# Contiguous step sizes, an earlier routing chain, and a bias table built inside the expert loop of a one-core decoder layer

## The chip, the cores and the metric

The kernel runs on one core of a Trainium2 chip. TensorE (PE) multiplies, VectorE (DVE), ScalarE (ACT) and GpSimd (POOL) do the elementwise work, and 16 DMA engines move data between device memory and the on-chip memory; SyncE (SP) issues most transfers, GpSimd the indirect ones (gather and scatter by row number). Each engine works through its own queue in order and waits at the head of it. The metric is the device time of one execution in microseconds (us), as the median of several runs.

## The reference

One decoder layer over 512 tokens of width 1024. A projection feeds a state-space branch (S5: 32 groups of 64 complex states, whose step sizes are exp of `ssm_log_step`, one number for each group) and a pooling branch with windows 2, 4, 8 and 16; both are gated, merged, projected, and added to the input in a layer norm. Then follow a mixture of 32 experts, 4 for each token, and a per-layer embedding:

```python
step = jnp.exp(log_step.astype(f32))[:, None]
lam_bar = jnp.exp(lam * step)
...
logits = (t @ w_router + b_router).astype(jnp.float32)
top_val, top_idx = lax.top_k(logits, TOP_K)
weights = jax.nn.softmax(top_val, axis=-1)
...
g = xb @ w_gate[e] + b_gate[e]
u = xb @ w_up[e] + b_up[e]
g = jnp.minimum(g, SWIGLU_LIMIT)
u = jnp.clip(u, -SWIGLU_LIMIT, SWIGLU_LIMIT)
glu = g * jax.nn.sigmoid(SWIGLU_ALPHA * g)
return ((u + 1.0) * glu) @ w_down[e] + b_down[e]
...
ple = jax.nn.sigmoid(h @ w_ple_gate[i]) * (p[i] @ w_ple_proj[i])
h = _layer_norm(DEEPNORM_ALPHA * h + moe_out + ple, ln2_g[i], ln2_b[i])
```

## The kernel before

The program has three stages. Ahead of the expert loop the order of each engine's queue is made at compile time by the tile framework's scheduler: it plays the program through with its own estimates of durations and gives each engine, whenever it is free, the ready instruction that comes first in the program's text. On the chip that order is fixed, and an instruction whose operand is late holds everything behind it. From `with tc.manual_schedule():` on (the expert loop) each engine keeps the order of the text among the loop's own instructions; where these fall among the instructions written before the loop is still the scheduler's choice.

**Front.** The 1024 x 3072 input projection and the other weights of this stage are loaded as 512 KB tiles (`load_raw`), and each tile is split into a high and a low half (`split`: the high half on ScalarE, the difference on VectorE, L104), so that three matmuls (`mm3`, L115 to L117) give nearly full precision. Line 167 loads the step sizes `lsb`: two transfers, each for 64 partitions, in which partition p of half g2 gets elements g2, g2+2, g2+4, ... of the 32 numbers. On VectorE a chain of some hundred small instructions on the tile `sm` makes the recurrence's coefficients from `par` and `lsb`. GpSimd makes tables of powers (`eb`, `er`, `ei`, L286 to L291) from them, VectorE uses these in the scan (`q_state`), and between them VectorE makes the pooling branch's `ph` (`pool_vec`), which PE multiplies at once.

**Routing and embedding.** After the output projection, each of four token tiles is normalized (`ln_vec`), stored to device memory as `hd`, and transposed into `hTs` (`ln_T`; tiles `ahi`, `alo`). `route_mm` makes the router's logits, `route_vec` transposes them (L764), adds the bias (`lg`, L767), finds the top four, ranks the experts by load (`key`, `cmp`, `col`), and makes the list row of every (token, choice), `ri` (L813). GpSimd writes 16 indirect scatters (L817) into the lists `lst`, and five loads bring these back as `ls` and `ls4` (L997, L1000). `ix4` (L1003) turns `ls4` into row numbers for the later scatter-adds. `route_cols` finds which expert has which rank (`eid`), makes `ib` (L855), and gathers the bias rows of all experts with four indirect transfers (L859) into `br`, from which ScalarE and VectorE make the table `btab` (L863, L864). Meanwhile PE computes the embedding in two halves of 512 columns: `ple_g` (L922 to L924) and L1079 to L1081 for the gate, `ple_p` (L939 to L941) for the projection; `ple_w` and `ple_wp` load and split its weights, VectorE multiplies and adds (`ple_mul`, `base_b`, `base_out`), and L957 stores the sum to `acc_d`.

**Expert loop.** 32 experts in a fixed order of their rank, each with three weights of 4 MB in four tiles of 1 MB; tile k of the stream goes into slot k of a ring of 16:

```python
ring += [(p_, "eraw", 1) for p_ in (ra, rb, rd, rg, rc, rf, re_)] + [(mtop, "eraw", 4)] * 4
...
for n in range(NR):
    do_load(n)
for i in range(2):
    gather(xgs[i], ls[:, i], CAP[i])
```

Five slots have memory of their own; the other eleven reuse memory of the stages before, so that their first load waits for the last instruction that reads the old tile. The four of `mtop` lie where `hTs` was. An expert's tokens are gathered from `hd` by the list (L1016), transposed (`half_T`, L1009, L1010) and multiplied (L1125). The bias comes from one matmul with `btab` (L1208): for the first expert behind its fourth weight tile, for the others ahead of the first. Results go by scatter-add to `acc_d` (L1160). The last expert is combined on PE, and the final layer norm closes the program.

Of the kernel before, what the change touches and what calls it, by code (L numbers as in the profile page):

```python
# [26 lines left out]
GP = G // 2  # L27
# [10 lines left out]
NB = 4  # L38
# [30 lines left out]
def _layer(top, tc, nc, x, xT, pT, ssm, ssm_d, log_step, w_in, w_val, w_glg, w_pg, pscale, w_pp,  # L69
# [96 lines left out]
    for g2 in range(2):  # L166
        nc.sync.dma_start(lsb[g2 * 64:(g2 + 1) * 64],
                          bass.AP(tensor=log_step.tensor, offset=log_step.offset + g2, ap=[[0, 64], [2, GP]]))
    dsk = sp.tile([32, GP], F32, name="dsk")
# [591 lines left out]
    def route_vec():  # L761
# [50 lines left out]
        V.tensor_reduce(rk, o2, axis=AX.X, op=OP.add)  # L812
        V.tensor_copy(ri, rk)  # L813
        scat = []
        for t_ in range(4):
            for k in range(K):
# [4 lines left out]
                scat.append(q_)  # L821
        tt(o2, oh, b4(wk), OP.mult)
        V.tensor_reduce(m1, o2.rearrange("p t k e -> p t e k"), axis=AX.X, op=OP.add)
# [5 lines left out]
    eid = late.tile([1, E], I32, name="eid")  # L829
    ib = mide.tile([128, 2], I32, name="ib")  # L830
    rowb = mide.tile([1, 2, NB, E], BF16, name="rowb")

    def route_cols():
# [21 lines left out]
        V.tensor_copy(ib, pb[:, 0:4].rearrange("p (h a) -> p h a", a=2)[:, :, 0])  # L855
        for h_ in range(2):
            br = mid.tile([128, 512], F32, tag="sg", name="br", bufs=4)
            for m_, b_ in enumerate((b_gate, b_up)):
                P.indirect_dma_start(out=br[:, m_ * 256:(m_ + 1) * 256], out_offset=None, in_=b_.rearrange("e (j c) -> (e j) c", j=NB),  # L859
                                     in_offset=bass.IndirectOffsetOnAxis(ap=ib[:, h_:h_ + 1], axis=0),  # L860
                                     bounds_check=NB * E - 1, oob_is_err=False)
            bh_ = mide.tile([128, 512], F32R, tag="bh", name="bh", bufs=1)
            S.copy(bh_, br)  # L863
            stt(btab[:, :, h_], bh_.bitcast(F32).rearrange("p (m c) -> p m c", m=2), odd, br.rearrange("p (m c) -> p m c", m=2), OP.mult, OP.add)  # L864

# [45 lines left out]
    def ple_w(n0):  # L911
        PW[n0] = [wtile(w_pleg, 2 * i, 2, n0 * 512, 512, P if n0 == 0 and i in (1,) else None) for i in range(4)]

# [62 lines left out]
    ple_g(0, 1)  # L976
    ln_T(3)
    route_mm()
    ple_g(0, 2)
    route_vec()  # L980

# [20 lines left out]
    ix4 = late.tile([128, NB, E], I32, name="ix4")  # L1002
    ts(ix4, ls4[:, :, :, 0], float(NB), OP.mult, jc, OP.add)  # L1003

# [15 lines left out]
    ple_g(0, 3)  # L1020
    route_cols()
    cn = mide.tile([128, 4, NB, E], BF16, name="cn")
    for r_ in range(NB):
        V.tensor_copy(cn[:, :, r_], mk)
    NC_ = N_CAND
# [27 lines left out]
    for t_ in range(4):  # L1053
        ple_p(0, t_, sacc())
        ple_mul(0, t_)
    ple_w(1)
    ple_wp(1)
    route_w()
# [145 lines left out]
    def bias(m_, c):  # L1204
        def f(os, start=True, stop=False):
            for i in range(len(os)):
                n_ = min(2, CAP[c] // 32 - 2 * i)
                TE.matmul(os[i][:, :256 * n_], lhsT=SL[c], rhs=btab[:, m_, c // 16, None, :].to_broadcast([128, n_, 256]),  # L1208
                          start=start, stop=stop, skip_group_check=True)
        return f  # L1210

    def raw_load(src, q_, down):
# [157 lines left out]
    with tc.manual_schedule():  # L1370
        for n in range(NR):
            do_load(n)
        for i in range(2):
            gather(xgs[i], ls[:, i], CAP[i])
        X[0] = x_tile()
        SL[0] = sel_e(0)
        for i in range(2):
            half_T(xgs[0], X[0], i, CAP[0], (S.copy, V.tensor_copy)[i])
        P.indirect_dma_start(out=tab, out_offset=bass.IndirectOffsetOnAxis(ap=bx[:NC_, 0:1], axis=0),
                             in_=bx[:NC_, 1:3], in_offset=None, bounds_check=NC_ - 1, oob_is_err=False)  # L1380
        n = 0
        for i in range(E + 1):
            for s in range(12):
# [4 lines left out]
                if i == E and s == 2:  # L1388
                    gb = tail_load(fin)
                if here:  # L1390
                    _, m_, q_ = seq[n]
                    w_ = raws.pop(n)
                    if m_ == 2:
                        c = ORD[i - 1]
                        last = i == E
                        if q_ == 0:
                            PY[c] = [acc(), acc()] if last else [sacc() for _ in banks(c)]
                        if last:
                            mm_rows(PY[c], HT[c], w_, q_, CAP[c])
                        else:  # L1400
                            mm_tile(PY[c], HT[c], w_, q_, nb_of(c), True, True)
                    else:
                        c = ORD[i]
                        os = (PG, PU)[m_][c]
                        mm_tile(os, X[c], w_, q_, nb_of(c), i == 0)
                        if i == 0 and q_ == 3:
                            bias(m_, c)(os, False, True)
                    do_load(n + NR)
                    n += 1
# [89 lines left out]
def _lay_out(inp):  # L1499
# [10 lines left out]
    r["ssm_d"] = c(a["ssm_d"].reshape(GP, 2, H).transpose(1, 2, 0).reshape(2 * H, GP))  # L1510
    r["log_step"] = c(a["ssm_log_step"].reshape(G))
    r["pool_scale"] = c(a["pool_scale"].reshape(4, 128).T)
# [17 lines left out]
```

## Time and profile before

| | |
|---|---|
| median of 3 runs (lowest, highest) | 1517.55 us (1516.02, 1518.83) |
| the profiled execution | 1518.69 us, span 1517.0 us |
| TensorE busy | 1356.2 us (89%) |
| VectorE, ScalarE, GpSimd busy | 438.2, 245.5, 287.7 us |
| read from and written to device memory | 453.23 MB, 17.80 MB |
| mean granted TensorE clock | 0.97 |

The span runs from the first to the last instruction in the trace; the execution's own time is 1.7 us longer. In the rows below, times are in us from the span's start, and a second number is a duration. `tile<-tiles` names what an instruction writes and reads, x5 counts merged instructions, and brackets hold the idle time of the engine before it and what ended that. PE, PEld, DVE, ACT, POOL are TensorE's matmuls and weight loads, VectorE, ScalarE, GpSimd; SPq and POOLq are the queues that issue transfers. A row of windows gives the stretch, its length, the busy time of PE, PEld, DVE, ACT and POOL, then the granted TensorE clock, the busy share of the DMA engines and GB/s. A row of waits gives the total, the number and the longest.

### The profile page before, as it was taken

To read this page: it belongs to the slowest core of one execution; us is meant where nothing else is said; L and a number is where in the kernel's file an instruction comes from. 1 tells how busy PE (TensorE), PEld (TensorE's weight loads), DVE (VectorE), ACT (ScalarE), POOL (GpSimd) and SP (SyncE) were. 2 spreads that over 40 slices of the span, in tenths; PEclk is the share of its full clock that TensorE was granted. 3 is DMA by queue.
4 is the path that set the end of the run, shared out by engine and by line. 5 is a ranking of instruction groups with operands and counts; after the bars stand their busy time and mean duration, and the time that the engine had idled before them with its cause. 6 is when DMAs were issued, how large, how long until landed. Compare 5 with 4: busy or idle time off the path is not lost.

```text
span 1517.0 us, 41208 instructions
## 1 busy us (share of the span) xinstructions
PE 1356.2 (89%) x18454; PEld 877.0 (58%) x18454; DVE 438.2 (29%) x940; ACT 245.5 (16%) x436; POOL 287.7 (19%) x293
## 2 busy tenths in 40 slices
PE   6779999999699999998989889989898899999993
PEld 6658887777455666554545445545454455556651
DVE  3986747587311111110111111101110111111106
ACT  2434334242100011000010000000100000000011
POOL 0294310002501112111112111111121111110132
PEclk9889999999899999999999999999999999999997
DMA  4412325730599999999999999999999999999953
GB/s 153 136 55 72 93 85 201 210 126 24 220 403 398 397 400 385 386 399 397 395 400 393 393 386 392 401 394 394 393 393 391 382 391 400 397 383 408 409 181 140
DMA packets 107780, 468.58 MB, mean 309 GB/s; under 512 B 19757, under 2 KB 44785, under 8 KB 58448
## 3 DMA queue, kind: packets, MB, share of 16 engines
q1 hardware_dynamic: 90864, 446.12, 75.3%
q0 software_dynamic: 16736, 19.79, 6.0%
q8 instruction: 146, 2.39, 0.6%
q14 instruction: 34, 0.28, 0.0%
HBM read 453.23 MB, written 17.80 MB: 311 GB/s over the span
## 4 chain that ended last, share of the span: by engine, by line
DMA 56%; PE 30%; DVE 5%; issue 4%; POOL 3%; ACT 0%; SPq 0%; DVEq 0%; ACTq 0%; POOLq 0%
DMA eraw<-in_w_down_dram 23%; DMA eraw<-in_w_up_dram 15%; DMA eraw<-in_w_gate_dram 14%; PE acc L1125 10%; PE ss L1125 5%; PE acc L116 3%; PE acc L117 3%; PE acc L115 3%; DMA lsb<-in_log_step_dram 2%; POOL lst L817 1%; PE acc L1132 1%; PE tp L1141 1%; DMA raw<-in_w_out_dram 1%; DMA lst<-dfl 1%; DVE eraw L191 1%
## 5 line engine op out<-in xcount | busy, mean ns | idle before, releaser
L1125 PE MATMUL acc<-eraw,xt 128*32 128x256 f32 x10880 | 608.7, 382 | 47.8 <-DMA eraw<-in_w_up_dram 45.4
L1125 PEld LDWEIGHTS acc<-eraw,xt 128*32 128x32 f32 x10880 | 347.2, 110 | 297.1 <-DMA eraw<-in_w_up_dram 65.8
L1125 PE MATMUL ss<-eraw,ht 128*32 128x256 f32 x5312 | 303.1, 383 | 31.4 <-DMA eraw<-in_w_down_dram 31.4
L1160 POOL DMA_INDIRECT acc_d<-y,ix x83 | 129.5, 1560 | 868.8 <-ACT y L1194 852.9
L1125 PEld LDWEIGHTS ss<-eraw,ht 128*32 128x32 f32 x5312 | 171.5, 111 | 158.6 <-DMA eraw<-in_w_down_dram 45.2
L1142 ACT COPY ht<-tp 128x512 f32<-128x512 f32 (+1 forms) x50 | 23.9, 516 | 649.9 <-PE tp L1141 649.9
L181 DVE TENSOR_SCALAR g<-acc 128x512 f32<-128x512 f32 (+1 forms) x51 | 30.6, 602 | 286.7 <-PE acc L1125 276.2
L1010 DVE COPY xt<-tp 128x384 f32<-128x384 f32 (+2 forms) x32 | 16.4, 511 | 332.1 <-PE tp L1009 332.0
L183 DVE TENSOR_SCALAR u<-acc 128x512 f32<-128x512 f32 (+1 forms) x51 | 30.6, 600 | 274.0 <-PE acc L1125 265.4
L115 PE MATMUL acc<-ahi,hi 128*128 128x512 f32 x160 | 64.3, 402 | 15.1 <-DVE sm L191 15.1
L1175 ACT ACTIVATE s<-g 128x512 f32<-128x512 f32 (+1 forms) x51 | 27.9, 559 | 282.4 <-DVE g L181 282.4
L104 DVE TENSOR_TENSOR lo<-raw,hi 128x1024 fp32r<-128x1024 f32 (+1 forms) x52 | 63.0, 1215 | 28.8 <-ACT hi L103 28.5
L103 ACT CAST hi<-raw 128x1024 fp32r<-128x1024 f32 (+1 forms) x53 | 54.9, 1036 | 72.6 <-PE acc L116 48.8
L117 PE MATMUL acc<-ahi,lo 128*128 128x512 f32 x160 | 63.9, 399 | 0.0
L116 PE MATMUL acc<-alo,hi 128*128 128x512 f32 x160 | 63.7, 398 | 0.0
L115 PEld LDWEIGHTS acc<-ahi,hi 128*128 128x128 f32 x160 | 31.0, 194 | 21.6 <-ACT hi L103 15.4
L1016 POOL DMA_INDIRECT xg<-hd,ls x32 | 32.4, 1014 | 34.4 <-PE tp L1009 24.9
L117 PEld LDWEIGHTS acc<-ahi,lo 128*128 128x128 f32 x160 | 30.8, 192 | 6.6
L116 PEld LDWEIGHTS acc<-alo,hi 128*128 128x128 f32 x160 | 30.9, 193 | 6.2
L1194 ACT ACTIVATE y<-ss,ls 128x256 f32<-128x256 f32 x83 | 33.8, 481 | 0.0
L187 DVE TENSOR_TENSOR g<-g,s 128x512 f32<-128x512 f32 (+1 forms) x51 | 29.2, 600 | 13.1 <-ACT s L1175 13.1
L191 DVE SCALAR_TENSOR_TENSOR u<-u,g 128x512 f32<-128x512 f32 (+1 forms) x51 | 30.8, 603 | 1.7
(404 smaller groups left out, 1301.3 us busy)
## 6 DMA issues: line engine op xcount, KB each, us to landing
eraw<-in_w_gate_dram SPq DMA_DIRECT2D x128, 1024.0 KB
eraw<-in_w_up_dram SPq DMA_DIRECT2D x128, 1024.0 KB
eraw<-in_w_down_dram SPq DMA_DIRECT2D x128, 1024.0 KB
raw<-in_w_in_dram SPq DMA_DIRECT2D x23, 512.0 KB
raw<-in_w_out_dram SPq DMA_DIRECT2D x8, 512.0 KB
raw<-in_w_ple_gate_dram SPq DMA_DIRECT2D x8, 512.0 KB
raw<-in_w_pool_proj_dram SPq DMA_DIRECT2D x4, 512.0 KB
raw<-in_w_glu_val_dram SPq DMA_DIRECT2D x4, 512.0 KB
```

The lines of the kernel that those rows point to most:

```text
L103: S.copy(h, v)
L104: (lo_eng or V).tensor_tensor(l, v, h.bitcast(F32), op=OP.subtract)
L115: TE.matmul(o, lhsT=lh, rhs=rh, start=start, stop=False)
L116: TE.matmul(o, lhsT=lh, rhs=rl, start=False, stop=False)
L117: TE.matmul(o, lhsT=ll, rhs=rh, start=False, stop=stop)
L181: V.tensor_scalar(o, i, a, None, op0=op)
L183: V.tensor_scalar(o, i, a, b, op0=op, op1=op1)
L191: V.scalar_tensor_tensor(o, a, s, b, op0=op0, op1=op1)
L1016: P.indirect_dma_start(out=xg[:n_], out_offset=None, in_=hd, in_offset=bass.IndirectOffsetOnAxis(ap=lst_[:n_, 0:1], axis=0), bounds_check= ...
L1125: TE.matmul(os[b // 2][j * 32:(j + 1) * 32, b % 2 * 256:b % 2 * 256 + 256], lhsT=x_, rhs=w_[:, kk, j * 256:(j + 1) * 256], start=first and ...
L1160: q_ = P.indirect_dma_start(out=acc_d.rearrange("t (j c) -> (t j) c", j=4), out_offset=bass.IndirectOffsetOnAxis(ap=ix_[b], axis=0), in_=y ...
L1194: S.activation(y_[:, b * 256:(b + 1) * 256], py[b // 2][:, c_], AF.Copy, scale=w_.bitcast(F32))
```

## The change

`log_step` is stored as two rows of 16 on the host, so that each partition loads one contiguous row. `ln_T(3)`, `route_mm` and `route_vec` get the highest priority of the scheduler. `route_vec` ends with the scatters; its former last part (the weights of each choice for the down bias) becomes `route_w3`. What VectorE does for `route_w3`, `route_cols`, the copies `cn` and the second half of the embedding's weights is ordered behind `ri`. Two of the four low halves of these weights, up to now all VectorE's, go to GpSimd. The bias gathers and `btab` move from `route_cols` into the first step of the expert loop, in two larger tiles of the loop's own memory; `ib` moves to a pool that lives on, and one buffer of 2 KB for each partition is gone. `ix4` moves from ahead of the embedding's rest into the loop's text, behind the first gathers.

```diff
--- before.py
+++ after.py
@@ -164,8 +164,7 @@
     nc.sync.dma_start(par, ssm)
     lsb = sp.tile([128, GP], F32, name="lsb")
     for g2 in range(2):
-        nc.sync.dma_start(lsb[g2 * 64:(g2 + 1) * 64],
-                          bass.AP(tensor=log_step.tensor, offset=log_step.offset + g2, ap=[[0, 64], [2, GP]]))
+        nc.sync.dma_start(lsb[g2 * 64:(g2 + 1) * 64], bc(log_step[g2], 64))
     dsk = sp.tile([32, GP], F32, name="dsk")
     nc.sync.dma_start(dsk, ssm_d)
 
@@ -810,7 +809,8 @@
         tt(o2, oh, rv[:, :, None, :].to_broadcast([128, 4, K, E]), OP.mult)
         rk = mide.tile([128, 4, K], F32, name="rk")
         V.tensor_reduce(rk, o2, axis=AX.X, op=OP.add)
-        V.tensor_copy(ri, rk)
+        RT["ri"] = V.tensor_copy(ri, rk)
+        RT["m1"], RT["wk"] = m1, wk
         scat = []
         for t_ in range(4):
             for k in range(K):
@@ -819,7 +819,11 @@
                 for o_ in scat:
                     tc.declare_no_dep(q_.ins, o_.ins, reason="each (token, choice) has a list row of its own")
                 scat.append(q_)
-        tt(o2, oh, b4(wk), OP.mult)
+
+    def route_w3():
+        o2, oh = (RT["s"][:, i].rearrange("p (t k e) -> p t k e", t=4, k=K) for i in range(2))
+        m1, wk = RT["m1"], RT["wk"]
+        tt(o2, oh, wk[:, :, :, None].to_broadcast([128, 4, K, E]), OP.mult)
         V.tensor_reduce(m1, o2.rearrange("p t k e -> p t e k"), axis=AX.X, op=OP.add)
         S.copy(w3[:, :, 0], m1)
         S.copy(w3[:, :, 2], m1)
@@ -827,7 +831,7 @@
         RT["w3"] = w3
 
     eid = late.tile([1, E], I32, name="eid")
-    ib = mide.tile([128, 2], I32, name="ib")
+    ib = late.tile([128, 2], I32, name="ib")
     rowb = mide.tile([1, 2, NB, E], BF16, name="rowb")
 
     def route_cols():
@@ -853,15 +857,6 @@
         for h_ in range(2):
             TE.matmul(pb[:, 2 * h_:2 * h_ + 2], lhsT=ir.rearrange("p e j a -> p (e j a)")[:, h_ * 128:(h_ + 1) * 128], rhs=one[0:1, 0:2], start=True, stop=True)
         V.tensor_copy(ib, pb[:, 0:4].rearrange("p (h a) -> p h a", a=2)[:, :, 0])
-        for h_ in range(2):
-            br = mid.tile([128, 512], F32, tag="sg", name="br", bufs=4)
-            for m_, b_ in enumerate((b_gate, b_up)):
-                P.indirect_dma_start(out=br[:, m_ * 256:(m_ + 1) * 256], out_offset=None, in_=b_.rearrange("e (j c) -> (e j) c", j=NB),
-                                     in_offset=bass.IndirectOffsetOnAxis(ap=ib[:, h_:h_ + 1], axis=0),
-                                     bounds_check=NB * E - 1, oob_is_err=False)
-            bh_ = mide.tile([128, 512], F32R, tag="bh", name="bh", bufs=1)
-            S.copy(bh_, br)
-            stt(btab[:, :, h_], bh_.bitcast(F32).rearrange("p (m c) -> p m c", m=2), odd, br.rearrange("p (m c) -> p m c", m=2), OP.mult, OP.add)
 
     def route_w():
         pt = tps()
@@ -909,7 +904,7 @@
     PW = {}
 
     def ple_w(n0):
-        PW[n0] = [wtile(w_pleg, 2 * i, 2, n0 * 512, 512, P if n0 == 0 and i in (1,) else None) for i in range(4)]
+        PW[n0] = [wtile(w_pleg, 2 * i, 2, n0 * 512, 512, P if i in ((1,), (0, 1))[n0] else None) for i in range(4)]
 
     def ple_g(n0, t_):
         c_ = slice(t_ * 128, (t_ + 1) * 128)
@@ -974,10 +969,11 @@
     ple_g(0, 0)
     ln_T(2)
     ple_g(0, 1)
-    ln_T(3)
-    route_mm()
+    with tc.high_priority():
+        ln_T(3)
+        route_mm()
+        route_vec()
     ple_g(0, 2)
-    route_vec()
 
     rn = [0]
 
@@ -1000,7 +996,6 @@
         P.dma_start(ls4[j * 32:(j + 1) * 32].rearrange("s b e w -> s b (e w)"),
                     lst[:128 * E].rearrange("(b s e) w -> s b (e w)", s=32, e=E))
     ix4 = late.tile([128, NB, E], I32, name="ix4")
-    ts(ix4, ls4[:, :, :, 0], float(NB), OP.mult, jc, OP.add)
 
     def half_T(src, o_, q_, n_=128, cp=S.copy):
         pt = tps()
@@ -1018,10 +1013,13 @@
                              bounds_check=T - 1, oob_is_err=False)
 
     ple_g(0, 3)
-    route_cols()
+    with tc.issue_after(RT["ri"].ins):
+        route_w3()
+        route_cols()
     cn = mide.tile([128, 4, NB, E], BF16, name="cn")
-    for r_ in range(NB):
-        V.tensor_copy(cn[:, :, r_], mk)
+    with tc.issue_after(RT["ri"].ins):
+        for r_ in range(NB):
+            V.tensor_copy(cn[:, :, r_], mk)
     NC_ = N_CAND
     cps = tps()[:NC_, :2]
     ones2 = one[:, 0:2]
@@ -1053,8 +1051,9 @@
     for t_ in range(4):
         ple_p(0, t_, sacc())
         ple_mul(0, t_)
-    ple_w(1)
-    ple_wp(1)
+    with tc.issue_after(RT['ri'].ins):
+        ple_w(1)
+        ple_wp(1)
     route_w()
     og = [acc() for _ in range(4)]
     order = (0, 1, 2, 3)
@@ -1208,6 +1207,21 @@
                 TE.matmul(os[i][:, :256 * n_], lhsT=SL[c], rhs=btab[:, m_, c // 16, None, :].to_broadcast([128, n_, 256]),
                           start=start, stop=stop, skip_group_check=True)
         return f
+
+    def bias_rows():
+        br = mz.tile([128, D], F32, tag="u2", name="br", bufs=2).rearrange("p (h m c) -> p h m c", h=2, m=2)
+        for h_ in range(2):
+            for m_, b_ in enumerate((b_gate, b_up)):
+                P.indirect_dma_start(out=br[:, h_, m_], out_offset=None, in_=b_.rearrange("e (j c) -> (e j) c", j=NB),
+                                     in_offset=bass.IndirectOffsetOnAxis(ap=ib[:, h_:h_ + 1], axis=0),
+                                     bounds_check=NB * E - 1, oob_is_err=False)
+        return br
+
+    def bias_table(br):
+        bh_ = mz.tile([128, D], F32, tag="y", name="bh", bufs=2).rearrange("p (h m c) -> p h m c", h=2, m=2)
+        S.copy(bh_.bitcast(F32R), br)
+        for h_ in range(2):
+            stt(btab[:, :, h_], bh_[:, h_], odd, br[:, h_], OP.mult, OP.add)
 
     def raw_load(src, q_, down):
         r = raw_tile()
@@ -1372,10 +1386,12 @@
             do_load(n)
         for i in range(2):
             gather(xgs[i], ls[:, i], CAP[i])
+        ts(ix4, ls4[:, :, :, 0], float(NB), OP.mult, jc, OP.add)
         X[0] = x_tile()
         SL[0] = sel_e(0)
         for i in range(2):
             half_T(xgs[0], X[0], i, CAP[0], (S.copy, V.tensor_copy)[i])
+        br = bias_rows()
         P.indirect_dma_start(out=tab, out_offset=bass.IndirectOffsetOnAxis(ap=bx[:NC_, 0:1], axis=0),
                              in_=bx[:NC_, 1:3], in_offset=None, bounds_check=NC_ - 1, oob_is_err=False)
         n = 0
@@ -1387,6 +1403,8 @@
                 hooks(i, s)
                 if i == E and s == 2:
                     gb = tail_load(fin)
+                if i == 0 and s == 2:
+                    bias_table(br)
                 if here:
                     _, m_, q_ = seq[n]
                     w_ = raws.pop(n)
@@ -1508,7 +1526,7 @@
     cc = [a[f"ssm_c_{s}"].reshape(GP, 2, H, PS).transpose(1, 3, 0, 2).reshape(128, GP * H) for s in ("re", "im")]
     r["ssm"] = c(np.concatenate(lam + b + cc, axis=1))
     r["ssm_d"] = c(a["ssm_d"].reshape(GP, 2, H).transpose(1, 2, 0).reshape(2 * H, GP))
-    r["log_step"] = c(a["ssm_log_step"].reshape(G))
+    r["log_step"] = c(a["ssm_log_step"].reshape(GP, 2).T)
     r["pool_scale"] = c(a["pool_scale"].reshape(4, 128).T)
     for k in ("w_in", "w_glu_val", "w_glu_gate", "w_pool_group", "w_pool_proj", "w_out", "ln1_g", "ln1_b",
               "w_router", "b_router", "w_gate", "b_gate", "w_up", "b_up", "w_down", "b_down", "w_ple_gate",
```

## Rows read from the trace of the kernel before

**Rows 1.** The chain that ended last, whole run: start, length, work.

```profile
12.92 24.12 DMA lsb<-in_log_step_dram
...
278.79 8.91 DMA lst<-dfl
...
364.84 1.18 POOL lst L817
...
385.85 5.07 DMA lst<-pay,ri
```

**Rows 2.** Windows of the late part: busy time of each engine, granted clock, DMA.

```profile
398.30:412.40 14.10, 13.13 (x55) 10.44 (x55) 9.12 (x15) 3.88 (x7) 6.42 (x9) 0.82 0.39 127
...
411.00:469.00 58.00, 55.90 (x946) 33.72 (x949) 11.18 (x24) 3.76 (x8) 3.86 (x5) 0.97 1.01 401
...
469.00:1363.00 894.00, 814.76 (x13900) 477.64 (x13888) 116.11 (x222) 81.31 (x182) 138.26 (x98) 0.99 1.02 393
```

**Rows 3.** SyncE's queue, 340 to 480 us, who waited for whom.

```profile
SPq L1217 <- PE tp L1009: 30.1, 1, 30.1
```

**Rows 4.** Who waited for whom, 0 to 125 us.

```profile
DVE sm L183 <- DMA lsb<-in_log_step_dram: 18.5, 1, 18.5
...
PE acc L115 <- DVE sm L191: 15.1, 1, 15.1
...
PE tp L116 <- DVE ph L187: 11.4, 1, 11.4
```

**Rows 5.** VectorE's timeline, routing stage: start, length, line, tiles, idle time before.

```profile
349.49 0.29 DVE L187 TENSOR_TENSOR lg<-tp,brt 128x128 f32<-128x128 f32 x1 [7.45 <-PE tp L764]
...
352.32 1.22 DVE L104 TENSOR_TENSOR lo<-raw,hi 128x1024 fp32r<-128x1024 f32 x1
...
360.88 1.22 DVE L187 TENSOR_TENSOR cmp<-cmp,ie 128x1024 f32<-128x1024 f32 x1
...
363.73 0.16 DVE L813 CAST ri<-rk 128x16 int32<-128x16 f32 x1
...
396.12 0.33 DVE L183 TENSOR_SCALAR ix<-ls,jc 128x128 int32<-128x128 int32 x1 [13.93 <-DMA ls<-lst]
```

**Rows 6.** VectorE's timeline in the front.

```profile
37.14 0.17 DVE L183 TENSOR_SCALAR sm<-lsb 128x16 f32<-128x16 f32 x1 [18.51 <-DMA lsb<-in_log_step_dram]
...
45.30 0.68 DVE L161 COPY v_u<-acc 128x512 f32<-128x512 f32 x1
```

**Rows 7.** TensorE's timeline in the front.

```profile
30.65 0.40 PE L117 MATMUL acc<-hi,alo 128*128 128x512 f32 x1
```

**Rows 8.** The page's 40 slices of the span, TensorE's busy tenths.

```profile
PE   6779999999699999998989889989898899999993
```

**Rows 9.** ScalarE's timeline, routing stage.

```profile
345.51 0.58 ACT L759 COPY rs<-tp 64x512 f32<-64x512 f32 x1 [4.30 <-PE tp L756]
```

**Rows 10.** TensorE's timeline, 336 to 372 us.

```profile
349.00 0.46 PE L764 MATMUL tp<-ident,rs 64*128 64x64 f32 x4
```

**Rows 11.** All engines' timeline, 318 to 325 us.

```profile
320.46 2.39 POOL L104 TENSOR_TENSOR lo<-raw,hi 128x1024 fp32r<-128x1024 f32 x1 [43.58 <-DVE lni L183]
...
320.93 1.93 DVE L187 TENSOR_TENSOR lnwk<-lni 128x1 f32<-128x1 f32 x1
...
324.79 0.15 DVE L187 TENSOR_TENSOR lnwk<-lnwk 128x1 f32<-128x1 f32 x1
```

**Rows 12.** TensorE's timeline, 372 to 424 us.

```profile
398.30 0.80 PE L939 MATMUL tp<-wp,pth 128*128 128x512 f32 x1 [13.45 <-DVE h L191]
...
409.39 0.39 PE L1081 MATMUL acc<-hi,alo 128*128 128x512 f32 x1
...
412.43 10.82 PE L1125 MATMUL acc<-eraw,xt 128*32 128x256 f32 x192
```

**Rows 13.** GpSimd's timeline, 318 to 420 us.

```profile
397.30 1.25 POOL L859 DMA_INDIRECT br<-in_b_gate_dram,ib  x1 [0.30 <-DVE h L187]
```

**Rows 14.** VectorE's timeline, 383 to 440 us.

```profile
404.95 0.75 DVE L191 SCALAR_TENSOR_TENSOR btab<-bh,odd,br 128x512 fp32r<-128x512 f32 x1 [1.24 <-ACT bh L863]
```

## The prediction

> **What bounds the kernel now.** I read the chain that ended last first, then the windows, then the waits of each engine. The chain [rows 1] names two early places where nothing else could go on. The load of the step sizes alone stands on it for 24.12 us from 12.92. Then come 16 list scatters on POOL, from 364.84 to the landing at 385.85 + 5.07 = 390.92. Behind them it is mostly the stream of expert weights, and the windows [rows 2] say why: from 411 to 1363 the DMA engines are full (1.01 and 1.02, 393 to 401 GB/s) while PE has 79 us of slack in the second window (894 less 814.76). So the loop's length is that of its weights, and what can be won lies before 411, the moment when the stream starts again. SyncE says what holds it until then: one load waited 30.1 us for PE [rows 3]. It waits for memory that the embedding's matmuls (names ahi, lo) still read; the ring's last slots come free only with them. Whatever moves the end of these matmuls (409.39 + 0.39 = 409.78, [rows 12]) and the first expert matmul (412.43) moves the end of the kernel, one for one.
>
> Two stages stand before that. In the front [rows 4] VectorE idles 18.5 us for the step sizes, PE idles 15.1 us behind that (its next operands are split on VectorE, in order), and 11.4 us once more for ph. In the routing stage VectorE's timeline [rows 5] shows the second knot: the first logits add at 349.49, the row numbers ri at 363.73, other work between them, and at 396.12 the one small row ix, before which VectorE stood 13.93 us for the lists. All the embedding's remaining work was queued behind ix: PE waits 13.45 us in turn [rows 12].
>
> **The change part by part. Step sizes.** 2 x 64 partitions x 16 elements are 2048 pieces of 4 bytes; 24.12 us is 11.8 ns for one. Now there are 128 rows of 64 bytes. No row shows such a load. From below: 128 x 11.8 ns = 1.5 us, landing at 14.4. From above: 128 rows of 2 KB took 8.91 us [rows 1], landing at 21.8. VectorE was ready for them at 37.14 - 18.51 = 18.63 [rows 6], so the wait left is 0 to 3.2 us; I take 0, since 64 bytes lie nearer to 4 than to 2048. The Trainium skill (DMA: Bandwidth & Descriptors, Specifications) wants 512 bytes or more for line rate, which 64-byte rows still miss; by it the load stays slow per byte, and the rival on a wait that stays is its case. That hangs on no number here.
>
> What takes the wait's place? VectorE's order has v_u, a copy of PE's first sums, 45.30 - 37.14 = 8.2 us behind the first use [rows 6]. It would come at 26.8, and PE's sums end at 30.65 + 0.40 = 31.05 [rows 7]: up to 4.2 us are lost if the order stays. From below the front gives 18.5 - 3.2 - 4.2 = 11.1 us. From above, PE's two waits go together, 15.1 + 11.4 = 26.5 us. I take 18.5: the two waits for POOL's products apart, VectorE works without a break from the step sizes to ph, where PE's second wait ends, and from the fourth of the page's 40 slices to the tenth PE is at 9 tenths [rows 8], so a shift there is kept.
>
> **Routing chain first.** The transposes of the logits start at 349.00 [rows 10] although their operand was ready at 345.51 + 0.58 = 346.09 [rows 9]; PE had embedding matmuls in between. Put first: 2.9 us. On VectorE, between 349.49 and 363.73, the change moves out two splits (1.22 busy, 1.13 from start to start; the second covered a wait for PE, so I count half), three passes over the 1024-wide comparison at 1.13 [rows 5] and three small copies (0.1 each): 1.1 + 0.6 + 3.4 + 0.3 = 5.4 us. Together 8.3 us. The moved work costs nothing where it goes: VectorE is idle from 382 to 396 and PE sets the pace.
>
> Against it: two of the second half's splits go from VectorE to POOL. The one split that POOL does now took 2.39 us [rows 11], and the 128 x 1 multiply that VectorE started in its midst took 1.93 us against 0.15 for its like. Two such meetings inside the routing chain cost up to 2 x 1.8 = 3.6 us, none cost nothing. The Trainium skill (SBUF — State Buffer, Who interferes with whom) has this as a rule: a VectorE instruction with two SBUF inputs and a GpSimd instruction that reads SBUF exclude each other. By it the chain loses the 3.6 us if both splits fall into it; the row agrees. I take 0.3, since the splits wait for buffers that embedding matmuls free late. So the lists come 8.0 us earlier, at 388.
>
> **Bias table.** Four gathers leave POOL's queue, two casts ScalarE's and two VectorE passes leave the stretch before the first expert. They cost the end nothing now: the embedding's matmuls on PE end at 409.78, after the table (404.95 + 0.75 = 405.70, [rows 14]). In the loop's first step the table is needed behind four weight tiles, 10.82 us after PE starts [rows 12]. Today's set takes from 397.30 [rows 13] to 405.70, 8.4 us; the cover holds if the gathers start no later than 2.4 us after PE does. They wait for memory that only embedding matmuls read, so they can. If late, PE loses that much, out of its slack. I count 0; losing the cover costs 0 to 8 us of PE and, for the end, what exceeds the loads already waiting, which I leave at 0 to 2.
>
> **The row ix.** It moves behind all embedding work in the program's text, but the compiler's scheduler still decides where it falls in VectorE's queue, and no row shows that. If it falls behind the embedding, the hold of VectorE goes, and with it at most PE's 13.45 us and the half-speed after it (granted clock 0.82 over 14.1 us, 2.5 us): 15.9 us, which then includes the 8.0. If it still falls in front, the embedding resumes when the lists land, and the stage gains just the 8.0 us. If it falls earlier, by as much as the routing chain moved forward, PE stands before more work: I put 4 us of the 8 back, which is 4. Bounds 3 and 15.9. I take 8.0, the middle case.
>
> Memory: the smaller pool shifts others by 2 KB; I count 0.
>
> **The sum.** 18.5 + 8.0 = 26.5 us. The profiled execution took 1518.69 us (span 1517.0 and 1.7 around it), which gives 1492.2; it stood 1.1 us above the median of 1517.55, so I forecast 1491 for the median.
>
> **Rivals.** (a) ix no longer holds anything: 18.5 + 15.9 = 34.4, 1483. For it: the new place in the text; against: the scheduler fills idle VectorE time, and lists that it takes as early stood in front this time too. (b) ix falls earlier: 18.5 + 4 = 22.5, 1495. For it: the routing chain, and with it the expected lists, move forward against the embedding. (c) PE's second front wait goes too: 26.5 + 8.0 = 34.5, 1483; against: POOL's part of the chain is no shorter. (d) The front wait is replaced (late 64-byte rows, v_u in front, another load): between 0 and 11 us, with 8.0 in the middle stage between 1498.5 and 1509.5. The step sizes then do not do what the change says. (e) Slower or level, by one mechanism: ix falls right behind ri, at 355.7. VectorE is then held until 388 with nearly all of the embedding behind it. PE has from 355.7 to 384.85 (29.2 us) and from 398.30 to 412.43 (14.1 us) of work left, so its experts start at 388 + 43.3 = 431.3, 18.9 us later than today; against 18.5 from the front that is 1518, and with PE also waiting for VectorE's 2 to 3 us of evacuations 1520 to 1521. It decides from there on: each us that ix falls later gives one back.
>
> **How the numbers follow.** Forecast 0.41, (a) 0.18, (b) 0.17, (c) 0.10, (d) 0.07, (e) 0.04, and 0.03 for gains that two new waits together eat up. Low end: 26.5 + 15.9 = 42.4, 1475. High end: 11.1 + 3 = 14.1, 1503.5. Inside lie the forecast, (a), (b), (c) and half of (d); the joint extremes and (e) are left out, under 2 in 10. This kernel can tell 0.2%, about 3 us, from no change: the forecast and (a) to (d) are faster, 0.93; same 0.03; (e) is the slower 0.04.
>
> **What would show it.** Right: no VectorE wait for lsb, PE without the gap at 31; ri about 9 us behind the first logits add (14.2 now); the lists near 370 and the first expert matmul near 386; the loop from the stream's start to the end as long as today. Wrong: a new wait at v_u or at a weight load near 30; a POOL split in front of the scatters; ix with more than 14 us of idle time before it; a bias matmul that PE waits for; or a loop that grows, which no term here allows for.

## The result and the profile after

The changed kernel takes 1494.65 us (median of 4 runs, 1493.64 to 1496.11) against 1516.86 us of the kernel before (4 runs): a ratio of 0.9852, 95% interval 0.9835 to 0.987, that is 22 us faster. The forecast was 1491.0 with 26.5 us of gain, the range 1475 to 1503.5. The profiled execution after took 1496.11 us, its span 1494.4.

The front first, VectorE's timeline of the changed kernel (start, duration, instruction, in brackets the idle time before it and what ended that); it answers to [rows 6]:

```profile
19.02 0.11 DVE L182 TENSOR_SCALAR sm<-lsb 128x16 f32<-128x16 f32 x1
...
27.12 0.68 DVE L161 COPY v_u<-acc 128x512 f32<-128x512 f32 x1
```

The first use of the step sizes has no wait in front of it and starts 18.1 us earlier. The copy v_u has none either. Of the waits [rows 4] only the last is left, as long as before (total, number, longest):

```profile
PE tp L116 <- DVE ph L186: 11.6, 1, 11.6
```

The routing chain on VectorE, in the order of [rows 5]:

```profile
326.61 0.29 DVE L186 TENSOR_TENSOR lg<-tp,brt 128x128 f32<-128x128 f32 x1 [4.74 <-PE tp L763]
...
334.53 2.02 DVE L186 TENSOR_TENSOR rs<-rs,rv 128x512 f32<-128x512 f32 x1
...
337.31 1.54 DVE L812 CAST ri<-rk 128x16 int32<-128x16 f32 x1
...
373.68 0.47 DVE L182 TENSOR_SCALAR ix<-ls,jc 128x128 int32<-128x128 int32 x1 [9.34 <-DMA ls<-lst]
```

From lg to ri it takes 10.7 us instead of 14.24. The product rs and the cast ri are slow here, 2.02 and 1.54 us. POOL shows why (its timeline), and also where the bias gathers now stand:

```profile
333.59 5.23 POOL L104 TENSOR_TENSOR lo<-raw,hi 128x1024 fp32r<-128x1024 f32 x2 [30.43 <-ACT hi L103]
339.14 1.37 POOL L817 DMA_INDIRECT lst<-pay,ri  x1 [0.32 <-DVE ri L812]
...
380.77 1.07 POOL L1215 DMA_INDIRECT br<-in_b_gate_dram,ib  x1 [0.32 <-issue]
```

The scatters start at 339.14, 25.7 us before the 364.84 of [rows 1]. VectorE still idles 9.34 us in front of ix, but all eight sums that free TensorE's banks now stand ahead of it. TensorE's timeline shows what follows; it answers to [rows 12]:

```profile
377.15 0.39 PE L1080 MATMUL acc<-hi,alo 128*128 128x512 f32 x1
...
380.76 10.57 PE L1124 MATMUL acc<-eraw,xt 128*32 128x256 f32 x192
400.90 1.01 PE L1207 MATMUL acc<-btab,sel_e 128*128 128x512 f32 x2 [9.57 <-DVE btab L190]
401.84 13.07 PE L1124 MATMUL acc<-eraw,xt 128*32 128x256 f32 x192
```

The wait of 13.45 us is gone, the embedding ends 32.2 us earlier and the first expert starts 31.7 us earlier. Then there is a new wait, 9.57 us for the bias table. The chain that ended last shows the same gathers as one of its pieces:

```profile
384.77 14.15 DMA br<-in_b_up_dram,ib
```

The last stretch starts where TensorE's chain switches from waiting for weights to its own work, at 1340.24 (1363.01 before): 22.8 us. So 31.7 us at the first expert became 22.8 at the end, and the first question is where the 9 us went. The wait of 9.57 us looks like the answer.

### The profile page after: what moved, and what is told of

Its sections match the earlier page's. It is cut to its first block, busy times and chain, and to the rows that moved or that the text cites. A ratio compares the mean times of both kernels' runs of the same rounds, so it can differ in the third digit from the quotient of the medians.

```text
span 1494.4 us, 41207 instructions
## 1 busy us (share of the span) xinstructions
PE 1354.0 (91%) x18454; PEld 874.6 (59%) x18454; DVE 439.3 (29%) x938; ACT 245.8 (16%) x435; POOL 292.5 (20%) x295
## 4 chain that ended last, share of the span: by engine, by line
DMA 51%; PE 35%; DVE 7%; POOL 4%; issue 2%; ACT 1%; SPq 0%; POOLq 0%; DVEq 0%; ACTq 0%
DMA eraw<-in_w_down_dram 17%; DMA eraw<-in_w_gate_dram 16%; DMA eraw<-in_w_up_dram 16%; PE acc L1124 13%; PE ss L1124 6%; PE acc L116 3%; PE acc L117 3%; PE acc L115 3%; POOL lst L817 1%; DMA br<-in_b_up_dram,ib 1%; PE acc L1131 1%; DVE h L190 1%; DVE lo L104 1%; PE acc L879 1%; PE tp L1140 1%
## 5 line engine op out<-in xcount | busy, mean ns | idle before, releaser
L1124 PE MATMUL acc<-eraw,xt 128*32 128x256 f32 x10880 | 615.5, 385 | 53.0 <-DMA eraw<-in_w_up_dram 50.0
L1124 PE MATMUL ss<-eraw,ht 128*32 128x256 f32 x5312 | 299.7, 380 | 23.0 <-DMA eraw<-in_w_down_dram 22.8
L1207 PE MATMUL acc<-btab,sel_e 128*128 128x512 f32 x102 | 28.3, 387 | 9.6 <-DVE btab L190 9.6
## 6 DMA issues: line engine op xcount, KB each, us to landing
eraw<-in_w_gate_dram SPq DMA_DIRECT2D x128, 1024.0 KB, 21.7
eraw<-in_w_up_dram SPq DMA_DIRECT2D x128, 1024.0 KB, 21.5
eraw<-in_w_down_dram SPq DMA_DIRECT2D x128, 1024.0 KB, 23.2
```

The lines of the kernel that those rows point to most:

```text
L1124: TE.matmul(os[b // 2][j * 32:(j + 1) * 32, b % 2 * 256:b % 2 * 256 + 256], lhsT=x_, rhs=w_[:, kk, j * 256:(j + 1) * 256], start=first and ...
```

## The experiments

**First group: the bias wait and the splits.** Theory 1: the wait for the bias table is paid at the end. Theory 2: from here on the weight stream alone sets the end, and the wait is TensorE's slack. A third question was what the two splits on POOL cost the routing chain.

The bias gathers moved ahead of the list loads on POOL (the rest of the old lines goes back as it was):

```diff
 def route_cols():
+    for h_ in range(2):
+        br = mid.tile([128, 512], F32, tag="sg", name="br", bufs=4)
+        for m_, b_ in enumerate((b_gate, b_up)):
+            RT["br"] = P.indirect_dma_start(out=br[:, m_ * 256:(m_ + 1) * 256], out_offset=None,
...
-ls = late.tile([128, E, 4], I32, name="ls")
-P.dma_start(ls.rearrange("p e w -> p (e w)"), lst[:128 * E].rearrange("(s e) w -> s (e w)", e=E))
...
     route_cols()
+    ls = late.tile([128, E, 4], I32, name="ls")
+    with tc.issue_after(RT["br"].ins):
+        P.dma_start(ls.rearrange("p e w -> p (e w)"), lst[:128 * E].rearrange("(s e) w -> s (e w)", e=E))
...
```

> The four bias gathers stand on POOL right behind the list scatters and in front of the list loads, into memory that the gate products leave free; casts and table passes follow in the embedding stage, and ix stays late. Theory 1 (the bias wait is paid at the end: 9.57 us of waiting on PE and 2.3 us of half speed behind it): the gathers start near 361.6, land before 372, PE runs from the first expert matmul near 381 without the gap before its first bias matmul, and the end comes 8 to 10 us earlier, 1485 to 1487. Theory 2 (from the expert stage on the weight stream alone sets the end, and PE's wait is slack): the gap goes as well but the time stays at 1493 to 1495.

Measured: 1496.8 us (0.9866, 0.9844 to 0.9889), no faster than the changed kernel. The wait itself went away. Each step of the loop has one small VectorE copy named sel_e at its beginning, so its starts are a clock of the loop. The changed kernel's timeline, the first, third, eleventh and last of the 32 copies:

```profile
379.54 0.22 DVE L1200 CAST sel_e<-sel 128x128 fp32r<-128x128 f32 x1
...
419.93 0.22 DVE L1200 CAST sel_e<-sel 128x128 fp32r<-128x128 f32 x1
...
666.92 0.22 DVE L1200 CAST sel_e<-sel 128x128 fp32r<-128x128 f32 x1
...
1385.68 0.22 DVE L1200 CAST sel_e<-sel 128x128 fp32r<-128x128 f32 x1
```

and the same four of this run:

```profile
382.31 0.22 DVE L1210 CAST sel_e<-sel 128x128 fp32r<-128x128 f32 x1
...
410.96 0.21 DVE L1210 CAST sel_e<-sel 128x128 fp32r<-128x128 f32 x1
...
666.49 0.22 DVE L1210 CAST sel_e<-sel 128x128 fp32r<-128x128 f32 x1
...
1386.04 0.22 DVE L1210 CAST sel_e<-sel 128x128 fp32r<-128x128 f32 x1
```

This run is 9.0 us ahead at the third, 0.4 at the eleventh, and 0.4 behind at the last. TensorE ran ahead of the weights and had to wait for them: 12.7 us between 420 and 700, against 4.8 in the changed kernel. Theory 1 has fallen.

The bias matmuls of the first expert left out (its output lacks its biases):

```diff
-if i == 0 and q_ == 3:
-    bias(m_, c)(os, False, True)
...
-if i == 0 and s == 2:
+if i == 0 and s == 10:
     bias_table(br)
```

> The bias matmuls of the first expert alone are left out (its output lacks its biases), and the table is made later in the first step, before the second expert needs it; the gathers stay where the change put them. Theory 1: with no wait before the first bias matmul the end comes 8 to 10 us earlier, 1485 to 1487, though gathers and stream still meet. Theory 2: 1493 to 1495, the loop is as long as its weights.

Measured: 1493.15 us (0.983, 0.9812 to 0.9848), 1.5 us below the changed kernel, within what can be told. Theory 2 again.

The bias table back where it was made before:

```diff
 def route_cols():
+    for h_ in range(2):
+        br = mid.tile([128, 512], F32, tag="sg", name="br", bufs=4)
...
+        stt(btab[:, :, h_], bh_.bitcast(F32).rearrange("p (m c) -> p m c", m=2), odd, br.rearrange("p (m c) -> p m c", m=2), OP.mult, OP.add)
...
-br = bias_rows()
...
-if i == 0 and s == 2:
-    bias_table(br)
```

> Only the bias table is put back where the kernel before made it, all else of the change stays. The gathers then stand on POOL behind the first row gathers and in front of the stores, near 377 to 382, and meet the full stream as well; VectorE takes the table passes in front of ix and of the first expert's operand copy. Theory 1: the wait moves ahead of the first expert matmul, which comes near 395 instead of 380.8; the end is level with the changed kernel or up to 5 us later, 1494 to 1500. Theory 2 (move of the table costs nothing either way): 1493 to 1495.

Measured: 1507.44 us (0.9925, 0.9908 to 0.9942), worse than either theory said. The table passes fell on VectorE in front of the last of the eight sums, VectorE waited 17.15 us for the gathers there, and the first step began at 393.31. So with the rest of the change in place, moving the table is worth 13 us, not because its work leaves the path but because its wait leaves VectorE's queue.

The two splits back on VectorE:

```diff
-        PW[n0] = [wtile(..., P if i in ((1,), (0, 1))[n0] else None) for i in range(4)]
+        PW[n0] = [wtile(..., P if n0 == 0 and i in (1,) else None) for i in range(4)]
```

> Only the two splits of the second half go back from POOL to VectorE. Theory P (VectorE and POOL exclude each other): the product before ri takes 0.7 us again (2.02 in the changed kernel), the cast 0.2 (1.54), and the scatters start 2.5 to 2.7 us earlier, near 336.5; the end gains what of it reaches the first expert and the bias gathers, 1 to 2.7 us, 1492 to 1493.5. Rival: the scatters start earlier but the end does not move, since the embedding's matmuls end where they did, 1494 to 1495.

Measured: 1508.93 us (0.9942, 0.9924 to 0.9959), 14 us slower; neither side had that. The chain itself did as theory P said (this run's VectorE timeline):

```profile
333.11 0.69 DVE L186 TENSOR_TENSOR rs<-rs,rv 128x512 f32<-128x512 f32 x1
...
334.56 0.17 DVE L812 CAST ri<-rk 128x16 int32<-128x16 f32 x1
...
371.26 0.33 DVE L182 TENSOR_SCALAR ix<-ls,jc 128x128 int32<-128x128 int32 x1 [18.30 <-DMA ls<-lst]
371.51 1.28 DVE L190 SCALAR_TENSOR_TENSOR h<-h,tp 128x512 f32<-128x512 f32 x2
```

2.02 became 0.69 and 1.54 became 0.17, and the scatters began 3.5 us earlier. But the compiler's scheduler now put ix in front of all eight sums h. VectorE stood 18.3 us, TensorE 10.7 us behind it, and the first step began at 394.51, 15 us late.

**Second group: where ix stands.** Theory X: the place of ix in VectorE's queue decides when TensorE and the weight slots go on.

The kernel before with the step sizes alone (and their two rows on the host's side, as in the change):

```diff
-        nc.sync.dma_start(lsb[g2 * 64:(g2 + 1) * 64],
-                          bass.AP(tensor=log_step.tensor, offset=log_step.offset + g2, ap=[[0, 64], [2, GP]]))
+        nc.sync.dma_start(lsb[g2 * 64:(g2 + 1) * 64], bc(log_step[g2], 64))
```

> The kernel before with the step sizes laid out in two rows and nothing else. If the front's gain is kept to the end, as the prediction counts it: everything from 37 us on comes 18.1 us earlier and the end too, 1498.5 to 1501. Rival (a part of it is lost again in the loop, as the changed kernel lost 3.5 of 26 us in its last steps): 1501 to 1504. What the changed kernel gains beyond this run is the worth of routing order, ix and bias table together, 4 to 8 us.

Measured: 1498.46 us (0.987, 0.9855 to 0.9885), 19.1 us faster than before. The front's gain is kept whole, and all the rest of the change brings just 3.8 us more by the medians. The two intervals overlap; in the traces the last step of the loop comes 4.5 us earlier.

The changed kernel with ix at its old place:

```diff
 ix4 = late.tile([128, NB, E], I32, name="ix4")
+ts(ix4, ls4[:, :, :, 0], float(NB), OP.mult, jc, OP.add)
...
-ts(ix4, ls4[:, :, :, 0], float(NB), OP.mult, jc, OP.add)
```

> The changed kernel with the row ix alone back at its old place in the text; it then falls ten instructions earlier on VectorE, in front of three of the first four sums that free PE's banks. Theory X (where ix stands decides when PE and the weight slots go on): VectorE is held until the lists land near 373, PE has a gap of some 10 us, the weight loads that wait for the embedding's slots go out 13 to 15 us later than at 378.9, and the end comes 12 to 15 us later, 1506 to 1510. Rival (the 14 us of the run with the splits back came from the splits themselves): 1494 to 1497.

Measured: 1509.37 us (0.9944, 0.993 to 0.9957), 14.7 us slower than the changed kernel. TensorE's timeline has the gap:

```profile
373.91 0.79 PE L945 MATMUL tp<-bdn,wdt 96*128 96x512 f32 x1 [13.90 <-DVE h L190]
```

Theory X holds; whether it also explains the 14 us of the splits is tested by the next run. The present one also says that the rest of the change, without moving ix, would have left the kernel 11 us behind the step sizes alone (4 of them are the weight slots, tested in the third group).

The splits back, and ix held behind the sums:

```diff
-        PW[n0] = [wtile(..., P if i in ((1,), (0, 1))[n0] else None) for i in range(4)]
+        PW[n0] = [wtile(..., P if n0 == 0 and i in (1,) else None) for i in range(4)]
...
-stt(hv, hv, _fl(ALPHA), o, OP.mult, OP.add)
+RT["bb"] = V.scalar_tensor_tensor(hv, hv, _fl(ALPHA), o, op0=OP.mult, op1=OP.add)
...
+with tc.issue_after(RT["bb"].ins):
     ts(ix4, ls4[:, :, :, 0], float(NB), OP.mult, jc, OP.add)
```

> The changed kernel with the two splits back on VectorE and ix told to stand behind the last of the eight sums of the embedding. Theory X: the 14 us that putting the splits back cost go away altogether, and as the lists and the embedding's own products come 3 to 5 us earlier without POOL's two splits beside the routing chain, the first expert starts near 376 to 378 and the end comes 2 to 5 us earlier than the changed kernel's, 1490 to 1493. Rival (the splits on VectorE are what delays PE): 1505 to 1509.

Measured: 1496.74 us (0.9863, 0.9848 to 0.9878). The 14 us are gone, as theory X said; the further 2 to 5 us did not come. The first step began at 382.30, behind the changed kernel's 379.54.

The same, with the small matmuls of ib later (RT["pp"] is the last matmul of ple_p):

```diff
+def route_ib():
+    ir = RT["ir"]
     pb = tps()
...
     ple_mul(0, t_)
+with tc.issue_after(RT["pp"].ins):
+    route_ib()
```

> The same as the run before it, and the two small matmuls that make the bias row numbers, for which PE waited 3.1 us near 342, stand behind the products of the embedding's projection. If PE's waits in this stage come off the end one for one: another 2 to 4 us, 1487 to 1490. Rival (the stream starts when the lists allow, or its slots come free no earlier): the same as the run before it.

Measured: 1497.0 us (0.986, 0.9845 to 0.9875), no gain; another wait of 4.7 us, for the split wp on ScalarE, took the place of the one removed.

**Third group: the rate of the stream.** If only the stream counts, two numbers of a trace must give the end: the bytes moved by 470 us, and those moved from 470 to 1300, when it always runs. The transfer view gives both; before:

```profile
DMA packets 39789, 73.64 MB, mean 157 GB/s; under 512 B 8882, under 2 KB 25906, under 8 KB 36012
...
DMA packets 54791, 326.71 MB, mean 394 GB/s; under 512 B 8562, under 2 KB 15018, under 8 KB 16626
```

and after:

```profile
DMA packets 39866, 85.01 MB, mean 181 GB/s; under 512 B 7354, under 2 KB 24602, under 8 KB 34757
...
DMA packets 54460, 324.04 MB, mean 390 GB/s; under 512 B 8522, under 2 KB 15010, under 8 KB 16632
```

The change leads by 11.37 MB at 470 us. At the loop's 0.3904 MB per us (324.04 MB in 830 us) that is 29.1 us. Then it loses 2.67 MB, 6.8 us, because its stream is slower. The difference, 22.3 us, is the shift of the last step (1408.45 less 1385.68 = 22.8). All runs follow, against before, one trace of each. The last four lines are those of the experiments further down:

| run | lead at 470, MB | in us | 470 to 1300, MB | in us | sum, us | last step earlier by, us |
|---|---|---|---|---|---|---|
| the change | 11.37 | 29.1 | -2.67 | -6.8 | 22.3 | 22.8 |
| bias_early | 10.48 | 26.8 | -1.93 | -4.9 | 21.9 | 22.4 |
| bias0_left_out | 9.78 | 25.1 | -1.40 | -3.6 | 21.5 | 21.7 |
| bias_back | 7.14 | 18.3 | -2.26 | -5.8 | 12.5 | 12.3 |
| splits_back | 6.06 | 15.5 | -1.83 | -4.7 | 10.8 | 10.2 |
| steps_only | 7.30 | 18.7 | -0.29 | -0.7 | 18.0 | 18.3 |
| ix_back | 5.56 | 14.2 | -1.93 | -4.9 | 9.3 | 8.8 |
| ix_late_splits_back | 10.72 | 27.5 | -1.88 | -4.8 | 22.6 | 22.7 |
| ix_and_rows_late | 10.45 | 26.8 | -2.41 | -6.2 | 20.6 | 21.2 |
| before_slots_off | -0.66 | -1.7 | -1.80 | -4.6 | -6.3 | -6.5 |
| slots_as_before | 10.97 | 28.1 | -0.65 | -1.7 | 26.4 | 27.4 |
| slots_all_on_64 | 9.83 | 25.2 | 0.60 | 1.5 | 26.7 | 27.4 |
| slots_all_on_512 | 10.11 | 25.9 | 1.95 | 5.0 | 30.9 | 32.4 |

In the first two groups every run built on the change lost 1.4 to 2.7 MB, and the one built on the kernel before lost 0.3. What they share is memory. The change takes ib (8 bytes a partition, 32 with rounding) from the pool "late" ahead of the weight tiles, and in the built program the first five of the sixteen weight slots begin at byte 32288 of each partition instead of 32256. The other eleven begin at 139232 and on in both. Theory A: where a slot begins sets the rate.

In the changed kernel, ib behind the slots:

```diff
-ib = late.tile([128, 2], I32, name="ib")
 ...
     pre_raw.append(r)
+ib = late.tile([128, 2], I32, name="ib")
```

> The changed kernel with the small tile ib taken from its memory pool behind the weight slots instead of in front of them. In the changed kernel the 8 bytes of ib (32 with rounding) push five of the sixteen weight slots from byte 32256 to 32288 and on, so that none of them begins on a multiple of 64 bytes any more; here they stand at 32256 again. Theory A (where the slots begin sets the rate of the weight stream: 393 to 394 GB/s in the two runs with five slots on multiples of 64, 390 to 392 in the eight with none): the rate from 470 to 1300 us goes back to 393 or 394 GB/s and the end comes 4 to 6 us earlier, 1488.5 to 1491. Rival (the rate differs by the order of the loads and stores in the loop): 390 to 392 GB/s, 1494 to 1497.

Measured: 1490.77 us (0.9813, 0.9798 to 0.9827), 3.9 us below the changed kernel, as theory A said.

The kernel before, with a pad ahead of them:

```diff
  eid = late.tile([1, E], I32, name="eid")
+late.tile([128, 8], F32, name="pad")
```

> The kernel before with 32 bytes of padding in front of its first five weight slots (32256 to 32288), so that they stand as in the changed kernel, and nothing else. Theory A: the stream falls from 394 to 390 to 392 GB/s and the kernel takes 4 to 6 us longer than before, 1521 to 1524. Rival: no difference, 1516 to 1519.

Measured: 1522.72 us, a ratio of 1.0027 (1.0017 to 1.0038). Padding that nothing reads makes the kernel before 4.6 us slower. These window rows from 700 to 1000 us, first before's and then this run's, have the rate in the last column:

```profile
700.00:1000.00 300.00, 266.34 (x4474) 152.45 (x4470) 38.16 (x74) 26.60 (x60) 40.54 (x29) 0.98 1.02 394
...
700.00:1000.00 300.00, 263.53 (x4456) 151.57 (x4449) 37.49 (x72) 24.20 (x54) 40.96 (x30) 0.99 1.02 391
```

The DMA engines are as full as before (1.02), and move less.

The run slots_as_before with a pad ahead of the other pools on the right side:

```diff
+    pad_.tile([128, 8], F32, tag="pad", name="pad", bufs=1)
```

> The run before it, and 32 bytes of padding that move the other eleven weight slots from multiples of 32 to multiples of 64 bytes (139232 to 139200 and so on). Theory A: if five of sixteen slots are worth 4 to 6 us, the other eleven are worth 9 to 13 more as long as the stream sets the end: 1476 to 1481, at 400 GB/s or more. Rival: the same as the run before it, or 1494 to 1497.

Measured: 1491.16 us (0.982, 0.9807 to 0.9834): no gain over the run with five slots moved, against theory A's 9 to 13 us. So theory A's price fails. But the run does not say that a multiple of 64 is worth nothing. By the table its rate rose, by 1.25 MB or 3.2 us, and its lead at 470 fell by 1.14 MB or 2.9 us. SyncE's queue shows where the lead went, in slots_as_before:

```profile
359.64 2.77 SPq L1231 DMA_DIRECT2D eraw<-in_w_up_dram  x3
362.45 0.45 SPq L1231 DMA_DIRECT2D eraw<-in_w_gate_dram  x1
```

and in this run:

```profile
357.58 0.83 SPq L1232 DMA_DIRECT2D eraw<-in_w_up_dram  x2
...
377.39 0.33 SPq L1232 DMA_DIRECT2D eraw<-in_w_up_dram  x1
377.76 1.99 SPq L1232 DMA_DIRECT2D eraw<-in_w_gate_dram  x3
```

The third of these loads now waits 19.3 us for a TensorE instruction (tp, L1004), so it and the load behind it, 1 MB each, go out some 15 us later. The pad also moves the loop's other tiles on that side (xt and y among them), so the eleven slots are not tested apart from these.

**All slots on 512.** The five slots begin on multiples of 512 (32256 is 63 x 512). The eleven lie 480 bytes past one before, 448 in the run above.

```diff
-pad_.tile([128, 8], F32, tag="pad", name="pad", bufs=1)
+pad_.tile([128, 120], F32, tag="pad", name="pad", bufs=1)
```

> The eleven other weight slots moved once more, by 480 bytes of padding, so that all sixteen begin on multiples of 512 bytes as the first five do (138752 and so on); all else as in the run with the slots as before. If what counts is a start on a multiple of 512 (the five that cost 4 us were moved off one, and the eleven that changed nothing at multiples of 64 lay at 448 of 512): the rate from 470 to 1300 us rises to 397 GB/s or more and the end comes 6 to 9 us earlier, 1482 to 1485. If 64 bytes already give all that there is to have, or the eleven slots do not matter: 393 to 395 GB/s and 1489 to 1492.

Measured: 1486.71 us (0.9793, 0.9779 to 0.9806), the fastest version of all. Its windows:

```profile
470.00:700.00 230.00, 224.18 (x3928) 136.75 (x3924) 31.61 (x60) 23.73 (x53) 37.61 (x27) 1.00 1.02 397
700.00:1000.00 300.00, 268.15 (x4533) 154.95 (x4526) 37.63 (x72) 25.15 (x56) 44.07 (x32) 0.99 1.02 398
1000.00:1300.00 300.00, 268.06 (x4519) 154.15 (x4520) 38.20 (x74) 26.04 (x59) 45.07 (x32) 0.98 1.02 393
```

The changed kernel has 391, 391 and 389 there. The rate rose to 397 and 398 as expected up to 1000 us, but is 396 over the whole stretch (328.66 MB in 830 us), and the gain of 4 us over slots_as_before is half of what was expected. Part of the rest went as in the run above: the third load again goes out at 377.49, and the lead at 470 is 0.86 MB or 2.2 us smaller than in slots_as_before, while the rate after it gives 2.60 MB or 6.7 us. Against slots_all_on_64, whose built program has the same instructions in the same order, the step from 448 to 512 gives 1.35 MB or 3.5 us by the rate; the intervals of the two ratios just fail to meet. Why the eleven slots give little more in the rate than the five did (2.60 against 2.02 MB) stays open.

## Why the prediction came out as it did

**Step sizes, 18.5 us: right.** 18.1 us in the trace, 19.1 us at the end when done alone. The 64-byte rows left no wait, and v_u did not take its place. The load in 4-byte pieces had also held SyncE's queue: the first and the third issue behind it took 4.92 and 9.40 us where the changed kernel has 0.58 and 0.50, and the later loads of the input weights start to go out at 15.55 instead of 28.58. What that is worth by itself no run tells. PE's second front wait stayed (11.6 us), as taken; rival (c) is out.

**Routing chain first, 8.0 us: the number nearly right, partly by luck, the way wrong.** The scatters begin 7.6 us earlier beyond the front, but two parts were mis-sized, in opposite directions. The first logits add came 4.8 us earlier beyond the front where I took 2.9; 1.2 of this steps_only has too. And both meetings with POOL's splits happened. They cost 2.02 - 0.69 and 1.54 - 0.17, so 2.7 us where I took 0.3 of at most 3.6. That is the side of the Trainium skill (SBUF — State Buffer, Who interferes with whom) that the prediction weighed; the trace agrees with it, and the page counts casts too among the instructions that can meet GpSimd there, under conditions. What failed is the step behind it, that the earlier lists bring the end forward by themselves. In ix_back they do not: ix comes 23.2 us earlier than before there (372.93), but TensorE needs 21.9 us from the end of its gap to the first step, against 13.5 before, and the last step comes 8.8 us earlier, where the step sizes alone give 18.3. That is the mechanism of rival (b), which I priced at 4 us.

**The row ix, middle case: wrong.** It stands in front of nothing that TensorE needs, which is rival (a), to which I gave 0.18. Its price was too high in turn. I put 15.9 us on it for the whole stage, from TensorE's waits; TensorE did gain 13.6 us beyond the front (31.7 less 18.1), but the stream gained 9.4 (28.1 less 18.7 us in the table, slots_as_before against steps_only). In steps_only some of the stream ran while TensorE stood: 181 GB/s from 365.6 to 379.5, its wait of 13.94 us, which is 2.5 MB or 6.4 us of the stream. So I forecast 8.0 from a case that did not happen, and the case that did was worth about as much.

**Bias table, 0 us: right at the end, wrong on the way.** The condition was met: the gathers start at 380.77, TensorE at 380.76. But the set of gathers, cast and passes took 8.4 us before and some 20 after, since the last gather landed 14.15 us after its issue beside the full weight stream. TensorE lost 9.57 us, and the end nothing, as "out of its slack" had it. What no term had is that leaving the table where it was would have cost this kernel 13 us (bias_back): the 0 holds for the table of the kernel before, not for the part that its move plays in the change.

**Memory, 0 us: this is the term that failed.** I saw a smaller pool shift others by 2 KB and counted 0. What shifts the weight slots is ib, by 32 bytes, and it costs 4 us: 1494.65 with it, 1490.77 without, and 4.6 us when done to the kernel before. Without that the forecast of 1491.0 would have been met to the microsecond, though partly by the exchange just told. "A loop that grows" stood on my list of what would show me wrong; it did.

## What to carry to other kernels

When a full stream of transfers sets the end, price a change by the bytes moved at a fixed time and by the rate after it; a wait of the compute engine is worth nothing there, even one that the chain that ended last runs through. An instruction that waits for a transfer holds all that stands behind it on its engine, so its place in the built program's queue must be looked at after every edit, also after edits that do not touch it (moving two splits moved ix and cost 14 us). And look at where the buffers of the stream begin before and after: a tile of 8 bytes in front of them cost as much as half of a stage's tuning gained.

## What the hardware showed that I had not expected

The start of a weight slot within its partition changes the rate of 1 MB loads at full DMA engines. With five of sixteen on multiples of 512 bytes 326.1 to 326.7 MB went through from 470 to 1300 us (327.3 where the other eleven lay on multiples of 64), with none 324.0 to 325.3, with all 328.7. For the five slots this is shown by itself; the eleven moved together with other tiles of the loop. Which multiple it takes no run tells: the starts on a multiple of 512 are multiples of 128 and 256 as well, and the others here are multiples of 32 or 64 at most. A cast of 128x16 with one input took 1.54 us beside a GpSimd split, 0.17 without.
